# Bonus and variance products of a gated SSM/RWKV block taken in high and low parts

## The chip, the cores and the metric

One core of a Trainium2 chip runs the whole kernel. The metric is device time in microseconds (us) of one execution; it is given as the median of the runs shown. The engines are named as in the profile: PE is TensorE's matmul side and PEld its weight loads, DVE is VectorE, ACT is ScalarE, POOL is GpSimd, and SP is the queue that issues most DMAs.

## The reference

One trunk layer on x of shape 1 x 2048 x 1024 in float32:

```
h = RMSNorm(x)
[u | rwkv_in | gate_a | gate_b] = h @ W_in
o_a = S5 diagonal SSM on u, then a half-GLU
o_b = RWKV-7 time mixing on rwkv_in            (8 heads x 64)
merged = sigmoid(gate_a)*(o_a @ Wb_a) + sigmoid(gate_b)*(o_b @ Wb_b)
x = x + merged @ W_out
x = x + relu(RMSNorm(x) @ W1)^2 @ W2
out = RMSNorm(x)
```

The change touches three sums over the 64 channels of a head inside o_b:

```
kk    = k*k_k / max(norm(k*k_k over the head), 1e-12)
var   = mean((y - mean)^2 over the head);  y = (y - mean)*rsqrt(var + 64e-5)
bonus = sum(r*k*r_k over the head) * v
```

## The kernel before, in words

The kernel runs in four phases: A (norm, input projection, S5), B (RWKV, and the two gate projections beside it), C (GLU, branch merge, output projection) and D (feed-forward). Only phase B (`phase_b`, from L600) is touched. Channels lie on the 128 partitions and time on the free axis; two heads share the partitions, so a sum over a head is a product with a 128x128 block matrix of ones: `bo` (ones) or `bo64` (ones divided by 64).

Phase B cuts the sequence into 16 pieces of 128 steps. For piece s there are three generators: `elem(s)` (L669) makes decays, the normalised key and the bonus; `inv(s)` (L760) makes the triangular inverse of each 64-step chunk, with a long run of small DVE steps (L805, L807) and a trip through DRAM; `chain(s)` (L878) carries the state and finishes the output. In turn i of the outer loop `robin` (L82) goes round chain(i-2), the gate projection, elem(i) and inv(i-1), one yield of each at a time. The gate projection (`gates`, L949) is a side generator: 64 output tiles of 24 products `gp`, each tile cut by yields into four portions of six products, so that they fill PE while the recurrence waits. Its weights are split into high and low parts on the chip in the first 16 tiles (ACT cast L963 to `gwh`, POOL subtraction L964 to `gwl`), stored, and read back for the other 48.

A generator's place in the round is its priority only. The framework's scheduler puts the instructions of each engine in an order at build time, taking the earliest one that its own simulation has ready; on the chip each engine then runs its list in that order, and waits where an input is late. `pin` (L666) forbids a matmul to be placed ahead of the PE instruction written before it. The SP queue, too, runs its DMAs in the order in which they stand.

The three sums before the change:

- The norm (L716 to L730): `sq` is the square of k*k_k. ACT casts it to the reduced float32 type `F32R` (`xh`, L721), POOL makes the rest `xl` (L722), and two unpinned products with `bor`, the cast of `bo`, add up in one PSUM bank `n` (L724, L725). DVE takes reciprocals of it (L728, L730), and from these come `AR` (L732) and, on POOL, `AG` (L736), which the first products `R` of chain (L893) read.
- The bonus (L742 to L749): DVE multiplies `rm` in four pieces (L743), and one full float32 product with `bo` follows in the same yield (L745); DVE multiplies the result by v (L749).
- The variance (L924 to L934): ACT copies and squares y (L924, L926); in the next yield one full float32 product with `bo64` (L929), the square root on ACT (L930), reciprocals on DVE (L931, L933). The end of chain multiplies by the gate and stores to `ob_d` through SP (L945).

Of the kernel before, what the change touches and what calls it, by code (L numbers as in the profile page):

```python
# [11 lines left out]
F32R = mybir.dt.float32r  # L12
# [3 lines left out]
ALU = mybir.AluOpType  # L16
# [583 lines left out]
def phase_b(tc, nc, K, io, pm_d, ob_d, h_d, gt_d, gs_d, inv_d):  # L600
    V, A, P, T = nc.vector, nc.scalar, nc.gpsimd, nc.tensor
    NS = S // 128
    with ExitStack() as st:
        gt = st.enter_context(tc.tile_pool(name="b_t", bufs=1, side="right", reuse_waits="tile"))
        gw = st.enter_context(tc.tile_pool(name="b_w", bufs=1, side="right", reuse_waits="tile"))
        cp = st.enter_context(tc.tile_pool(name="b_c", bufs=1, side="right", reuse_waits="tile"))
        ep = st.enter_context(tc.tile_pool(name="b_e", bufs=1, reuse_waits="tile"))
# [10 lines left out]
        def cst(n):  # L618
            o, w = COFF[n]
            return ct[:, o - NCST_A:o - NCST_A + w]  # L620

        bo, bo64, cent = cst("bo"), cst("bo64"), cst("cent")
        bor = cp.tile([128, 128], F32R, name="bor")
        A.copy(bor, bo)
        msi = cst("msi").rearrange("p (m t) -> p m t", m=2)
        lvl = cst("lvl").bitcast(U32)
# [18 lines left out]
        def gps(n):  # L645
            return psg.tile([128, 512], F32, tag="g", name=n)
# [16 lines left out]
        def fl(a):  # L663
            return a.rearrange("p h t -> p (h t)")

        def pin(f):  # L666
            return lambda *a, **k: tc.keep_in_program_order(f(*a, **k))

        def elem(s):  # L669
            d = D[s]  # L670
            if s == 0:
# [3 lines left out]
            rm, km, vm, sig, aa = (d[n] for n in ("rm", "km", "vm", "sig", "aa"))  # L675

            def tmp(n):
                return ep.tile([128, 4, 128], F32, tag=n, name=f"{n}{s}")
# [6 lines left out]
            kt, bt = BK[:, :, 0::3, :], BK[:, :, 1:3, :]  # L685
            sq = tmp("sq")
            A.activation(fl(sq), fl(kr), ACTF.Square)
            for _ in range(3):
                yield
            e1 = tmp("e1")  # L690
            V.tensor_tensor_scan(fl(e1), rst, fl(sig), 0.0, op0=ALU.mult, op1=ALU.add)
# [24 lines left out]
            d["AR"] = AR  # L716
            V.tensor_tensor(AR[:, :, 1, :], rm, e1, op=ALU.mult)
            np_ = gps(f"n{s}")
            xh = ep.tile([128, 512], F32R, tag="xh", name=f"xh{s}")
            xl = ep.tile([128, 512], F32R, tag="xl", name=f"xl{s}")  # L720
            A.copy(xh, fl(sq))  # L721
            P.tensor_tensor(xl, fl(sq), xh, op=ALU.subtract)  # L722
            yield
            T.matmul(np_, bor, xl, start=True, stop=False)  # L724
            T.matmul(np_, bor, xh, start=False, stop=True)  # L725
            P.tensor_tensor(sig, sig, kr, op=ALU.mult)
            V.scalar_tensor_tensor(fl(kr), fl(kr), -1.0, fl(e3), op0=ALU.mult, op1=ALU.mult)
            V.reciprocal(fl(sq)[:, 0:256], np_[:, 0:256])  # L728
# [6 lines left out]
            for c in range(2):  # L735
# [4 lines left out]
                            op=ALU.mult)  # L740
            yield
            for h in range(4):  # L742
                V.scalar_tensor_tensor(rm[:, h], rm[:, h], r_k[:, h:h + 1], km[:, h], op0=ALU.mult, op1=ALU.mult)  # L743
            bp = gps(f"bo{s}")
            T.matmul(bp, bo, fl(rm), start=True, stop=True)  # L745
            P.tensor_tensor(kt, km.rearrange("p h (c t) -> p h c t", c=2), e3.rearrange("p h (c t) -> p h c t", c=2),
                            op=ALU.mult)
            bv = xp.tile([128, 4, 128], F32, tag="bv", name=f"bv{s}", bufs=3)
# [129 lines left out]
        def chain(s):  # L878
# [3 lines left out]
            for c in range(2):  # L882
                n = 2 * s + c
# [14 lines left out]
                for h in range(8):  # L898
                    T.matmul(up[uc, 64 * h:64 * h + 64], Y[uc, h, :], R[uc, 64 * h:64 * h + 64],
                             start=True, stop=True)  # L900
# [16 lines left out]
                if n < 2 * NS - 1:  # L917
                    for e in range(2):
                        er = slice(64 * e, 64 * e + 64)
                        V.tensor_tensor(S1[er, :, er], SG[er], sp[er, 0:256].rearrange("p (h t) -> p h t", h=4),  # L920
                                        op=ALU.add)
# [2 lines left out]
            A.copy(ys, yp)  # L924
            y2 = ip.tile([128, 512], F32, tag="y2", name=f"y2{s}")
            A.activation(y2, yp, ACTF.Square)  # L926
            yield
            vp = gps(f"var{s}")
            T.matmul(vp, bo64, y2, start=True, stop=True)  # L929
            A.activation(y2, vp, ACTF.Sqrt, bias=geps)  # L930
            V.reciprocal(y2[:, 0:256], y2[:, 0:256])  # L931
            yield
# [73 lines left out]
        for i in range(NS + 2):  # L1006
            robin(chain(i - 2) if i >= 2 else None, gg, elem(i) if i < NS else None,
                  inv(i - 1) if 0 <= i - 1 < NS else None)
# [812 lines left out]
@with_exitstack  # L1821
def tile_hybrid_block(ctx: ExitStack, tc: tile.TileContext, io: dict, out: bass.AP):
    nc = tc.nc
    dp = ctx.enter_context(tc.tile_pool(name="dram", bufs=1, space=DRAM))
    u_d = dp.tile([512, 8, S // 8], F32, name="u_d")
    pm_d = dp.tile([2688, S], F32, name="pm_d")
    gt_d = dp.tile([2 * DM, S], F32, name="gt_d")
    h_d = dp.tile([2, NW, 128, NK, WT], F32, name="h_d")
    inv_d = dp.tile([S // 128, 2, 64, 256], F32, name="inv_d")
    gs_d = dp.tile([16, 2, 128, NK, 128], F32, name="gs_d")  # L1830
    z_d = dp.tile([512, 8, S // 8], F32, name="z_d")
    ob_d = dp.tile([512, S], F32, name="ob_d")
    oa_d = dp.tile([512, S], F32, name="oa_d")
    x1_d = dp.tile([S, DM], F32, name="x1_d")
    xt_d = dp.tile([3, 2, 128, 4, 512], F32, name="xt_d")
    r_d = dp.tile([16, 4, 128, 2, 512], F32, name="r_d")
    if True:
        K = setup(tc, nc, ctx, io)
        phase_a(tc, nc, K, io, u_d, pm_d, h_d, z_d)
        phase_b(tc, nc, K, io, pm_d, ob_d, h_d, gt_d, gs_d, inv_d)  # L1840
        with ExitStack() as sd:
            ff = []

            def following():
                ff.extend(ff_open(tc, nc, K, io, x1_d, xt_d, r_d, sd))
                return ff[1].ahead()

            phase_c(tc, nc, K, io, z_d, oa_d, ob_d, gt_d, x1_d, xt_d, following)
            phase_d(tc, nc, K, io, x1_d, r_d, out, *ff)
# [21 lines left out]
```

## Time and profile before

| | |
|---|---|
| median of 3 runs | 3075.23 us (3069.72 to 3085.65) |
| the profiled execution's own time | 3079.11 us |
| its span in the trace | 3077.3 us |
| mean granted TensorE clock | 0.979 of full speed |
| PE / PEld busy | 95% / 75% of the span |
| DVE / ACT / POOL busy | 61% / 36% / 40% of the span |
| phase B, from the first gate product to the last | about 557 to 1364 us |

Busy PE is not PE at its peak: a matmul's modelled duration overlaps the next one's, so what a product costs a full PE is read from the distance between starts in the timeline. Times in a timeline are microseconds from the start of the span; "[1.43 <-PE var L929]" says that the engine was idle for 1.43 us before the instruction, and what released it.

### The profile page before, as it was taken

Reading aid. Unit: us, or ns where it says so; the run is one execution under the profiler, and the core shown is the slowest. Engines: PE = TensorE matmul, PEld = TensorE weight load, DVE = VectorE, ACT = ScalarE, POOL = GpSimd, SP = SyncE. Lnnn points to the kernel's source line nnn. Section 1 sums busy time; section 2 is a strip of 40 time slices with the busy share of each in tenths; the row PEclk is TensorE's granted clock in tenths of the full one; section 3 lists DMA queues with packets and bytes.
Section 4 is the critical chain, followed back from the end, with each engine's and each line's share of the span. In section 5 each row is a group of like instructions: output and inputs, shape, how many; then the busy total and the mean of one; then the engine's idle time right before and its main releaser. Section 6 shows DMA issues by size and latency. Waiting matters only on the chain.

```text
span 3077.3 us, 45569 instructions
## 1 busy us (share of the span) xinstructions
PE 2913.9 (95%) x17024; PEld 2322.5 (75%) x17024; DVE 1892.2 (61%) x3307; ACT 1119.9 (36%) x1795; POOL 1219.9 (40%) x1069
## 2 busy tenths in 40 slices
PE   7989999589999999999999989999999999999998
PEld 5757777467777777777777868887788788888887
DVE  6348876457776677535323366657655476666667
ACT  5342211233333233234445355555433342222233
POOL 3101110545334333103333335555444555555554
PEclk9999999799999999999999999999999999999999
DMA  4344444756646545467565653333533386666664
GB/s 149 95 134 134 144 141 129 228 170 186 207 143 205 163 142 180 126 176 236 192 193 170 208 186 133 109 110 115 171 110 110 115 252 153 154 155 151 151 146 148
DMA packets 331676, 486.04 MB, mean 158 GB/s; under 512 B 113344, under 2 KB 174912, under 8 KB 331456
## 3 DMA queue, kind: packets, MB, share of 16 engines
q1 hardware_dynamic: 303296, 443.29, 45.1%
q0 software_dynamic: 11520, 35.66, 6.7%
q10 hardware_dynamic: 16640, 4.20, 0.5%
q8 instruction: 134, 2.20, 0.3%
q14 instruction: 86, 0.70, 0.1%
HBM read 327.71 MB, written 147.85 MB: 155 GB/s over the span
## 4 chain that ended last, share of the span: by engine, by line
PE 54%; DVE 10%; DMA 6%; issue 5%; POOL 3%; ACT 2%; SPq 1%; POOLq 0%; DVEq 0%; ACTq 0%
PE s L121 6%; PE s L123 6%; PE s L122 6%; PE f L121 5%; PE f L123 5%; PE f L122 5%; PE gp L121 2%; PE gp L122 2%; PE gp L123 2%; DMA g<-gt_d 1%; PE o L121 1%; PE o L122 1%; PE o L123 1%; DVE YC L807 1%; DVE bl L1331 1%
## 5 line engine op out<-in xcount | busy, mean ns | idle before, releaser
L121 PE MATMUL f<-bl,w1h 128*128 128x512 f32 x896 | 354.7, 396 | 8.9 <-ACT w1h L1358 8.9
L122 PE MATMUL f<-bh,w1l 128*128 128x512 f32 x896 | 351.0, 392 | 5.8 <-POOL w1l L1362 5.7
L123 PE MATMUL f<-bh,w1h 128*128 128x512 f32 x896 | 351.9, 393 | 0.0
L121 PE MATMUL s<-w2l,ah 128*128 128x512 f32 x784 | 305.8, 390 | 2.6 <-ACT s L1599 2.6
L123 PE MATMUL s<-w2h,ah 128*128 128x512 f32 x784 | 305.7, 390 | 0.0
L122 PE MATMUL s<-w2h,al 128*128 128x512 f32 x784 | 305.5, 390 | 0.0
L1362 POOL TENSOR_TENSOR w1l<-w1r,w1h 128x512 fp32r<-128x512 f32 x122 | 175.0, 1437 | 183.4 <-ACT w1h L1358 183.0
L121 PE MATMUL gp<-gh,gwh 128*128 128x512 f32 x512 | 222.4, 434 | 22.3 <-DMA gh<-h_d 13.5
L122 PE MATMUL gp<-gh,gwl 128*128 128x512 f32 x512 | 211.9, 414 | 10.5 <-POOL gwl L964 6.9
L1358 ACT CAST w1h<-w1r 128x512 fp32r<-128x512 f32 x224 | 137.8, 620 | 204.6 <-PE f L123 143.3
L1576 POOL TENSOR_TENSOR al<-ra,ah 128x1024 fp32r<-128x1024 f32 x64 | 166.9, 2610 | 111.5 <-ACT ah L1575 111.4
L123 PE MATMUL gp<-gh,gwh 128*128 128x512 f32 x512 | 209.6, 409 | 0.0
L1606 DVE TENSOR_TENSOR c<-c,s 128x512 f32<-128x512 f32 x224 | 149.8, 684 | 90.6 <-PE s L123 90.5
L122 PEld LDWEIGHTS f<-bh,w1l 128*128 128x128 f32 x896 | 169.2, 189 | 45.5 <-POOL w1l L1362 8.9
L121 PEld LDWEIGHTS f<-bl,w1h 128*128 128x128 f32 x896 | 169.3, 189 | 45.3 <-ACT w1h L1358 10.4
L123 PEld LDWEIGHTS f<-bh,w1h 128*128 128x128 f32 x896 | 169.1, 189 | 38.3
L121 PE MATMUL p<-hl,wh 128*128 128x512 f32 x448 | 182.6, 408 | 3.6 <-ACT lo L583 3.6
L123 PE MATMUL p<-hh,wh 128*128 128x512 f32 x448 | 178.3, 398 | 0.0
L122 PE MATMUL p<-hh,wl 128*128 128x512 f32 x448 | 177.8, 397 | 0.0
L121 PEld LDWEIGHTS s<-w2l,ah 128*128 128x128 f32 x784 | 147.6, 188 | 33.6 <-ACT s L1599 3.0
L122 PEld LDWEIGHTS s<-w2h,al 128*128 128x128 f32 x784 | 147.6, 188 | 30.8
L123 PEld LDWEIGHTS s<-w2h,ah 128*128 128x128 f32 x784 | 147.5, 188 | 30.7
(382 smaller groups left out, 6763.5 us busy)
## 6 DMA issues: line engine op xcount, KB each, us to landing
w1r<-in_w_dram SPq DMA_DIRECT2D x64, 512.0 KB, 3.4
r_d<-c SPq DMA_DIRECT2D x128, 256.0 KB, 2.0
ra<-r_d SPq DMA_DIRECT2D x64, 512.0 KB, 3.3
gwl<-gs_d SPq DMA_DIRECT2D x48, 512.0 KB, 4.5
gwh<-gs_d SPq DMA_DIRECT2D x48, 512.0 KB, 4.6
ch<-r_d POOLq DMA_DIRECT2D x42, 512.0 KB, 5.5
gh<-h_d SPq DMA_DIRECT2D x64, 256.0 KB, 5.4
gt_d<-gs SPq DMA_DIRECT2D x64, 256.0 KB, 5.1
```

Of the source, the lines that this page charges most:

```text
L121: nc.tensor.matmul(ps, wh, xl, start=start, stop=False)
L122: nc.tensor.matmul(ps, wl, xh, start=False, stop=False)
L123: nc.tensor.matmul(ps, wh, xh, start=False, stop=stop)
L807: V.tensor_tensor(YC[:, 0:k, k:16], YC[:, 0:k, k:16], tv, op=ALU.add)
L1331: V.tensor_tensor(l[k], o, h[k], op=ALU.subtract)
L1358: cast = A.copy(h, o)
L1362: (P if n % 2 or edge else V).tensor_tensor(l, o, h, op=ALU.subtract)
L1576: P.tensor_tensor(l, raw[n], h, op=ALU.subtract)
L1606: V.tensor_tensor(d, d, bank, op=ALU.add if i in (4, 5, 6) else ALU.subtract)
```

## The change

The float32 products of bonus and variance become pairs of `F32R` products like the norm's, with a second cast constant `bor64`. A helper `parts` makes the high part on ACT and the low part on DVE (the norm's low part moves from POOL to DVE), and a helper `ones` issues the two products, both pinned. The three users share one buffer each for `xh` and `xl`. In elem one of three early yields goes, and one is added between the bonus's parts and its product, so that elem still has 14 yields; the steps between the two run one yield earlier. In chain the parts come in the yield of the square.

```diff
+        bor64 = cp.tile([128, 128], F32R, name="bor64")
+        A.copy(bor64, bo64)
         A.copy(bor, bo)
...
+        def parts(n, x):
+            xh = ep.tile([128, 512], F32R, tag="xh", name=f"xh{n}")
+            xl = ep.tile([128, 512], F32R, tag="xl", name=f"xl{n}")
+            A.copy(xh, x)
+            V.tensor_tensor(xl, x, xh, op=ALU.subtract)
+            return xh, xl
+
+        def ones(ps, w, xh, xl):
+            pin(T.matmul)(ps, w, xl, start=True, stop=False)
+            pin(T.matmul)(ps, w, xh, start=False, stop=True)
...
-            for _ in range(3):
+            for _ in range(2):
                 yield
             e1 = tmp("e1")
...
-            xh = ep.tile([128, 512], F32R, tag="xh", name=f"xh{s}")
-            xl = ep.tile([128, 512], F32R, tag="xl", name=f"xl{s}")
-            A.copy(xh, fl(sq))
-            P.tensor_tensor(xl, fl(sq), xh, op=ALU.subtract)
-            yield
-            T.matmul(np_, bor, xl, start=True, stop=False)
-            T.matmul(np_, bor, xh, start=False, stop=True)
+            xh, xl = parts(f"n{s}", fl(sq))
+            yield
+            ones(np_, bor, xh, xl)
...
+            xh, xl = parts(f"b{s}", fl(rm))
+            yield
             bp = gps(f"bo{s}")
-            T.matmul(bp, bo, fl(rm), start=True, stop=True)
+            ones(bp, bor, xh, xl)
...
             A.activation(y2, yp, ACTF.Square)
+            xh, xl = parts(f"v{s}", y2)
             yield
             vp = gps(f"var{s}")
-            T.matmul(vp, bo64, y2, start=True, stop=True)
+            ones(vp, bor64, xh, xl)
```

## Rows read from the trace of the kernel before

**Rows 1.** The page: engine totals, then busy tenths of PE and its clock in 40 slices.

```profile
PE 2913.9 (95%) x17024; PEld 2322.5 (75%) x17024; DVE 1892.2 (61%) x3307; ACT 1119.9 (36%) x1795; POOL 1219.9 (40%) x1069
...
PE   7989999589999999999999989999999999999998
...
PEclk9999999799999999999999999999999999999999
```

**Rows 2.** Windows: length, busy us of PE, PEld, DVE, ACT, POOL; clock, DMA, GB/s.

```profile
560.00:580.00 20.00, 6.66 (x20) 3.12 (x18) 7.28 (x7) 5.93 (x9) 10.08 (x15) 0.76 1.08 334
580.00:600.00 20.00, 9.84 (x37) 7.06 (x37) 12.02 (x15) 5.49 (x9) 18.87 (x21) 0.72 0.34 119
...
900.00:950.00 50.00, 48.29 (x536) 38.12 (x536) 35.78 (x82) 17.79 (x32) 18.64 (x26) 1.00 0.56 158
950.00:1000.00 50.00, 49.47 (x524) 39.26 (x523) 35.60 (x61) 19.77 (x33) 17.11 (x23) 1.00 0.70 225
```

**Rows 3.** Groups by line, 560 to 1345 us: the products of the three sums.

```profile
L745 PE MATMUL bo<-rm,cstb 128*128 128x512 f32 x32 | 17.7, 636 | 3.3 <-DVE ys L944 2.2 <-DVE YC L807 0.6 <-DVE sq L730 0.4
...
L929 PE MATMUL var<-y,cstb 128*128 128x512 f32 x32 | 16.3, 591 | 0.0
...
L724 PE MATMUL n<-xl,bor 128*128 128x512 f32 x16 | 7.3, 456 | 5.2 <-POOL xl L722 5.2
```

**Rows 4.** Timeline of PE around one variance product, full clock.

```profile
951.75 0.39 PE L123 MATMUL gp<-gh,gwh 128*128 128x512 f32 x1
951.98 1.02 PE L929 MATMUL var<-y,cstb 128*128 128x512 f32 x2
952.43 0.79 PE L121 MATMUL gp<-gh,gwh 128*128 128x512 f32 x1
953.06 0.40 PE L122 MATMUL gp<-gh,gwl 128*128 128x512 f32 x1
953.30 0.39 PE L123 MATMUL gp<-gh,gwh 128*128 128x512 f32 x1
```

**Rows 5.** Groups of one tile: casts and subtractions into high and low parts.

```profile
L721 ACT CAST xh<-sq x16: 617/620/623, 569.2 to 1231.1; 128x512 fp32r<-128x512 f32 x16
...
L722 POOL TENSOR_TENSOR xl<-sq,xh x16: 1257/1502/2222, 569.9 to 1233.1; 128x512 fp32r<-128x512 f32 x16
...
L572 DVE TENSOR_TENSOR xl<-sg,xh x4: 680/692/692, 137.6 to 205.4; 128x512 fp32r<-128x512 f32 x4
```

**Rows 6.** Timeline of POOL and PE at the start of phase B.

```profile
569.92 2.22 POOL L722 TENSOR_TENSOR xl<-sq,xh 128x512 fp32r<-128x512 f32 x1 [17.63 <-ACT xh L721]
...
586.62 2.04 POOL L736 TENSOR_TENSOR AG<-AR,gam 128x512 f32<-128x512 f32 x2
588.63 2.34 POOL L964 TENSOR_TENSOR gwl<-gwr,gwh 128x1024 fp32r<-128x1024 f32 x1
...
587.71 1.33 PE L893 MATMUL R<-SB,AG 128*64 128x128 f32 x5 [14.30 <-POOL AG L736]
...
591.13 0.92 PE L122 MATMUL gp<-gh,gwl 128*128 128x512 f32 x1
...
607.47 1.16 PE L667 MATMUL m<-AR,BK 64*128 64x128 f32 x16
```

**Rows 7.** Waits of 560 to 1345 us: engine, line, awaited: us, times, longest.

```profile
DVE y L931 <- ACT y L930: 21.8, 5, 9.1
...
PE U L899 <- DVE Rs L895: 1.9, 4, 0.8
```

**Rows 8.** Timeline of the square root and the reciprocal behind it, one piece.

```profile
953.03 0.69 ACT L930 ACTIVATE y<-var,geps 128x512 f32<-128x512 f32 x1 [1.43 <-PE var L929]
...
954.49 1.74 DVE L931 RECIPROCAL y<-y 128x256 f32<-128x256 f32 x1
```

**Rows 9.** Timeline of DVE and POOL where a DVE step meets a POOL one.

```profile
731.80 2.30 DVE L805 TENSOR_TENSOR yt<-NC,YC 64x64 f32<-64x64 f32 x1
734.13 0.22 DVE L807 TENSOR_TENSOR YC<-YC,yt 64x64 f32<-64x64 f32 x1
...
731.63 2.39 POOL L964 TENSOR_TENSOR gwl<-gwr,gwh 128x1024 fp32r<-128x1024 f32 x1 [2.32 <-ACT gwh L963]
```

**Rows 10.** Timeline of the SP queue at the end of phase B.

```profile
1352.05 0.37 SPq L945 DMA_DIRECT2D ob_d<-ys  x1
1352.53 0.93 SPq L959 DMA_DIRECT2D gwh<-gs_d  x1
1353.50 0.45 SPq L959 DMA_DIRECT2D gwl<-gs_d  x1
```

## The prediction, made before the change was run

> **What bounds the kernel now.** I read the page first: PE is busy 95% of the span, in nearly every slice nine tenths or more, at a granted clock that is near full [rows 1]. So the question for each edit is whether it gives or takes time on PE. Then I cut phase B into windows. It has two parts. In its first 40 us PE works 6.66 and 9.84 us of 20 at a clock of 0.76 and 0.72, while POOL is busy 18.87 of 20 in the second window: here POOL sets the pace. Later, in the two windows from 900 to 1000, PE is busy 48.3 and 49.5 us of 50 at a clock of 1.00, DVE about 36, ACT 18 to 20, POOL 17 to 19 [rows 2]. There the gate products fill PE, so PE time that is saved is time of the kernel, and PE that waits costs the same.
>
> **What goes from PE.** A full float32 product shows as two records, so 16 pieces give 32 of them for each of bonus and variance, of 590 to 640 ns; the norm's half is one record of 456 ns [rows 3]. Records overlap, so I price by starts. Gate products of the same shape start 0.23 us apart (951.75 to 951.98; 953.06 to 953.30). The variance product starts at 951.98; the second gate product behind it starts at 953.06, and the first one's share of that is 0.23, so variance held PE from 951.98 to 952.83, or 0.85 us [rows 4]. Two reduced products hold it for 0.46. The saving is 0.39 us, times 32 products: **-12.5 us**. Where PE is idle anyway (the first window) it is worth nothing, but that touches one or two products of 32.
>
> **What is added elsewhere.** ACT gets 32 casts of 0.62 us, 20 us. DVE gets 48 subtractions of 0.69 us (priced by the same operation in phase A), 33 us, and POOL loses 16 of 1.50 us, 24 us [rows 5]. Neither ACT (18 to 20 of 50 busy) nor DVE (36 of 50) comes near being full by that: a piece takes some 44 us, as the 16 casts from 569.2 to 1231.1 show [rows 5], and DVE gains 2.1 us in each, so 36 of 50 becomes 38.4. Throughput hides these; the cover is PE's own work, and without it they would cost their own 33 us on DVE. The cast of the second constant is one small ACT instruction before the first gate product, where PE waits for loads: nothing. Nothing is added to or moved past the SP and POOL queues except as said below; the pieces issue the same DMAs.
>
> **The wait that is added.** In the norm and the variance PE now needs a low part that stands in DVE's list, behind whatever DVE was given before it, and PE stands still while it waits, with gate products behind it. The trace has no such wait for them: variance shows 0.0 idle, since only ACT stood ahead of it, and the norm's 5.2 is the one at the start [rows 3]. I bound it from rows in which PE does wait for DVE. Low end: the 32 products U behind Rs lost 1.9 us in all, 0.06 each [rows 7]. High end: how late DVE comes to work that is ready. At one piece the square root was done at 953.72 and DVE took it up at 954.49, 0.77 us later [rows 8]; in only 5 of 16 pieces did DVE wait for ACT there at all, so in the others it came late [rows 7]. Nearest is the bonus product itself, which already waits for DVE's multiply in its own yield: 3.3 us in 16, 0.21 each [rows 3]. I take 0.21 for the 32 norm and variance products: **+6.6 us** (1.9 to 25). The bonus keeps its 3.3: its parts come one yield earlier and its product stays where it was, with 1.3 us more work in a round of nearly 3 us (44 over 15 rounds). Moving the middle of elem one yield earlier changes no sum of work; a gain or a loss of a microsecond or two is possible, and I take zero. The shared buffers put the norm's cast behind the variance product of the piece two before it; before, it could run far ahead. That is inside the 0.21.
>
> **The start.** POOL runs without a gap from 569.92 to the low part of the second gate weights, 588.63 to 590.97, and the first gate product that reads it starts at 591.13. The norm's first low part, 2.22 us, lies in that run [rows 6] and goes: **-2.2 us**. Against it, the norm's products are now pinned behind the gate products written before them, so `AR` and `AG` come later; PE stood 14.3 us for `AG` anyway [rows 6], and the inverse's first products, which read `AR`, start only at 607.47 [rows 6]. Bounds for the stage: -4.3 us, if the gate weights now also pass the 2.04 us of `AG` in POOL's list, and +4 us, if the later `AG` is what PE meets next.
>
> **The end.** The last variance takes a cast and a subtraction more, 1.3 us, and 0.39 less on PE. The store of its output heads the SP queue, ahead of the last gate weights [rows 10], so **+0.9 us** passes on to the last gate products.
>
> **Sum.** -12.5 + 6.6 - 2.2 + 0.9 = -7.2 us. The profiled execution took 3079.1 us (its span and 1.8 around it); this makes it 3071.9. It is 3.9 above the median, and the same sum on the median of 3075.2 gives **3068**. A change of 0.5%, 15.4 us, is about what a measurement of this kernel can tell from none: the bounds are 3059.9 and 3090.6. With the waits at their low end and the start at its better end the sum is -14; with the waits three times as long and the start neutral it is +8. The main case's own range is 3061 to 3083.
>
> **A rule on the other side.** A DVE step on 64x64 took 2.30 us at 731.80 while a POOL subtraction ran from 731.63 for 2.39, and 0.22 us right after it [rows 9]. So a DVE instruction with two inputs can be held for most of a POOL one. The Trainium skill says why, SBUF — State Buffer, section SBUF: two separate sides: VectorE with two SBUF inputs and GpSimd share a port pair that one of them locks for a whole instruction. The row agrees. By that rule a subtraction that starts on DVE while POOL is at work waits for the rest of it, and moving it to DVE can hurt; this is the slower rival below.
>
> **The rivals.** *Slower:* the low parts are late, above all the variance's, which falls into the run of small DVE steps of inv that POOL stretches. Its price: if each of 48 products waits as long as in rows 8, 0.77 us, that is 37 us, less 12.5 and 2.2: +22, or 3097. It decides from (15.4 + 12.5 + 2.2) / 48 = 0.63 us a product. For it: DVE came late in 11 of 16 pieces [rows 7]. Against: one wait lets DVE catch up, so the next is shorter; 16 POOL subtractions that hold DVE go; and other products that need DVE lose far less. 0.17.
>
> *Faster:* waits stay at 0.06 each, as for U, 1.9 us, and the first stage of phase B, where PE idles on POOL, gives 4.3 us and the norm's second low part 1.3: -12.5 + 1.9 - 5.6 = -16, or 3059. For it: the idle time of the first windows is large [rows 2], and the list of POOL loses what stood in the way. Against: it needs each term at its good end. 0.27.
>
> *It shows nothing:* the change doesn't do what the price of a product says, because the order of the lists shifts and the 0.39 us comes back as waits somewhere: 3075, between 3068 and 3082. For it: the saving is 0.4% of the time, and the waits that take it need only be 0.4 us for each of 32 products. 0.22.
>
> **How the numbers follow.** The main case has 0.34, and lies within 0.5%, as does the third rival. Faster by over 0.5%: 0.27. Slower: 0.18, the rival and a hundredth for a worse start. Within: 0.55. The range reaches from 3052, past the centre of the faster case, to 3095, near the centre of the slower one; about 0.05 lies below and 0.12 above.
>
> **What would show it.** Bonus, variance and norm products of 390 ns in pairs, 16 of each half, with starts 0.23 us apart; POOL without its 16 subtractions; 48 DVE subtractions near 0.69 us. PE's waits for a low part between 2 and 10 us in all. The first gate product with the second low weights at 589 us or before. I am wrong if these waits pass 20 us, if the low parts take over 1 us on DVE on the average, or if the first stage moves by more than 5 us either way.

## The result, and the profile after

The median after the change is 3102.19 us (5 runs, 3094.35 to 3104.62), against 3075.23 before: a ratio of 1.0082, 95% interval 1.0066 to 1.0099. The kernel became slower by about 25 us (the ratio on 3075; the two medians lie 27 apart). The forecast was 3068 us, and 3102 lies above its range of 3052 to 3095.

The profiled execution took 3102.2 us, with a span of 3100.3 (before 3077.3). The page, as in [rows 1]:

```profile
PE 2926.5 (94%) x17024; PEld 2331.4 (75%) x17024; DVE 1917.5 (62%) x3355; ACT 1137.1 (37%) x1828; POOL 1217.6 (39%) x1053
...
PE   7989999589899999999999989999999999999998
...
PEclk9999999889999998999999999999999999999999
```

No engine got fuller by much: DVE went from 61% to 62%, ACT from 36% to 37%. PE is still the engine that bounds the kernel. Slices are 77.5 us long, and phase B lies in the 8th to the 18th: there its busy row has an 8 more (the 11th), and its clock row has 8 in three slices, where before it had one 7. (PE's count of records is the same, since a full product already showed as two.)

Where the 23 us of span come from is seen in the tile of the gate products, first and last start. The first two lines are the kernel before, the others the kernel after:

```profile
L121 PE MATMUL gp<-gh,gwh x512: 387/395/799, 556.6 to 1363.4; 128*128 128x512 f32 x171
L122 PE MATMUL gp<-gh,gwl x512: 387/393/918, 557.2 to 1363.6; 128*128 128x512 f32 x171
```

```profile
L121 PE MATMUL gp<-gh,gwh x512: 387/397/797, 557.9 to 1391.5; 128*128 128x512 f32 x171
L122 PE MATMUL gp<-gh,gwl x512: 386/394/795, 558.4 to 1391.8; 128*128 128x512 f32 x171
```

Phase B starts 1.3 us later and ends 28.1 us later (1391.5 against 1363.4); the phases behind it then take 5 us less. So all of it arises in phase B. Cut into four windows, with the columns of [rows 2], the kernel before:

```profile
610.00:800.00 190.00, 166.06 (x1572) 127.40 (x1571) 133.37 (x251) 64.36 (x105) 94.19 (x108) 0.92 0.60 189
800.00:1000.00 200.00, 194.79 (x2140) 153.76 (x2140) 144.47 (x289) 75.20 (x129) 79.58 (x110) 1.00 0.58 176
1000.00:1200.00 200.00, 188.44 (x1937) 144.44 (x1936) 142.92 (x310) 63.78 (x110) 78.24 (x109) 0.97 0.55 163
1200.00:1400.00 200.00, 193.50 (x1756) 151.18 (x1755) 107.34 (x204) 63.43 (x109) 38.45 (x35) 0.97 0.54 156
```

and the kernel after:

```profile
610.00:800.00 190.00, 161.80 (x1465) 121.34 (x1464) 133.68 (x250) 65.44 (x108) 86.78 (x96) 0.92 0.55 177
800.00:1000.00 200.00, 191.81 (x2173) 151.71 (x2170) 146.02 (x303) 75.99 (x133) 82.93 (x112) 0.99 0.59 175
1000.00:1200.00 200.00, 186.84 (x1845) 143.03 (x1845) 140.72 (x306) 70.62 (x122) 67.88 (x98) 0.96 0.50 149
1200.00:1400.00 200.00, 187.39 (x1807) 144.60 (x1806) 107.61 (x221) 55.17 (x101) 32.94 (x38) 0.93 0.49 147
```

Read the third number, PE's busy time, and the clock behind POOL's column. PE is busy 742.8 us of 790 before and 727.8 after: 15 us more idle. And its clock is lower in three of four windows, by 0.01, 0.01 and 0.04. Busy time times clock, window by window, is 718 us before and 692 after, so PE did about 26 us less work in the same stretch, 15 from standing still and the rest from the clock. (The last window of before holds some 36 us of the next phase.) The change made PE's work smaller; PE stood still more and ran slower.

The groups of the three sums, with the forms kept apart, 560 to 1385 us, answer to [rows 3] and [rows 5]. Behind the bar: busy us, mean ns of one, then the idle time of the engine just before them and what ended it.

```profile
L669 PE MATMUL var<-xlv,bor 128*128 128x512 f32 x16 | 7.8, 487 | 11.3 <-DVE xlv L676 11.3
L669 PE MATMUL n<-xln,bor 128*128 128x512 f32 x16 | 7.4, 463 | 7.4 <-DVE xln L676 7.0
L669 PE MATMUL bo<-xlb,bor 128*128 128x512 f32 x16 | 7.0, 437 | 1.9 <-DVE xlb L676 1.9
...
L676 DVE TENSOR_TENSOR xlb<-rm,xhb 128x512 fp32r<-128x512 f32 x16 | 14.8, 926 | 0.0
L676 DVE TENSOR_TENSOR xlv<-y,xhv 128x512 fp32r<-128x512 f32 x16 | 10.9, 680 | 10.6 <-ACT xhv L675 10.6
L676 DVE TENSOR_TENSOR xln<-sq,xhn 128x512 fp32r<-128x512 f32 x16 | 10.4, 649 | 1.3 <-ACT xhn L675 1.3
...
L675 ACT CAST xhb<-rm 128x512 fp32r<-128x512 f32 x16 | 9.9, 620 | 32.1 <-PE n L669 31.6 <-DVE y L946 0.6
```

The products are cheap, as said, and the subtractions are near 0.68 us. What is new stands in the last column of the first line: the variance product, which showed 0.0 idle before [rows 3], now waits 11.3 us for its low part. The last line shows the shared buffer: in all, ACT stands 31.6 us before the bonus's casts until the norm's product has let the buffer go. PE's largest waits of the same stretch, as in [rows 7], read line, awaited, total, times, longest:

```profile
PE gp L121 <- ACT gwh L976: 18.5, 3, 12.1
PE gp L122 <- POOL gwl L977: 13.6, 5, 8.1
PE var L669 <- DVE xlv L676: 11.3, 11, 3.6
PE n L669 <- DVE xln L676: 7.0, 3, 4.0
```

The first two, 32.1 us, belong but for 0.5 us to the first 110 us of phase B. There they take the place of the 14.3 us for `AG` and the norm's 5.2 [rows 3, rows 6], and of 13.3 for the same two in the kernel before: 32.8 in all. One variance product in the timeline of ACT, DVE and PE, at full clock:

```profile
959.60 0.60 ACT L938 ACTIVATE y<-y 128x512 f32<-128x512 f32 x1
960.24 0.62 ACT L675 CAST xhv<-y 128x512 fp32r<-128x512 f32 x1
...
961.64 0.39 PE L123 MATMUL gp<-gh,gwh 128*128 128x512 f32 x1
...
962.01 0.21 DVE L819 TENSOR_TENSOR YC<-YC,yt 64x60 f32<-64x60 f32 x1
962.15 0.68 DVE L676 TENSOR_TENSOR xlv<-y,xhv 128x512 fp32r<-128x512 f32 x1
...
962.88 0.50 PE L669 MATMUL var<-xlv,bor 128*128 128x512 f32 x1 [0.85 <-DVE xlv L676]
...
963.22 0.39 PE L669 MATMUL var<-xhv,bor 128*128 128x512 f32 x1
...
963.45 0.40 PE L121 MATMUL gp<-gh,gwh 128*128 128x512 f32 x1
```

The cast is done at 960.86. DVE is in the small steps of `inv` and takes the subtraction at 962.15, 1.3 us later. PE issued its last gate product at 961.64 and stands 0.85 us, with gate products behind the variance in its list that need nothing from DVE. This repeats in 11 of 16 pieces.

### The profile page after: what moved, and what is told of

Read it like the earlier page. It is cut to its first block, busy times and chain, and to the rows that moved or that the text cites. A ratio compares the mean times of both kernels' runs of the same rounds, so it can differ in the third digit from the quotient of the medians.

```text
span 3100.3 us, 45670 instructions
## 1 busy us (share of the span) xinstructions
PE 2926.5 (94%) x17024; PEld 2331.4 (75%) x17024; DVE 1917.5 (62%) x3355; ACT 1137.1 (37%) x1828; POOL 1217.6 (39%) x1053
## 4 chain that ended last, share of the span: by engine, by line
PE 51%; DVE 7%; DMA 5%; issue 4%; POOL 3%; ACT 2%; SPq 1%; POOLq 0%; DVEq 0%; ACTq 0%
PE f L121 6%; PE f L123 6%; PE f L122 6%; PE s L122 6%; PE s L123 6%; PE s L121 6%; DMA g<-gt_d 2%; PE gp L121 2%; PE gp L122 1%; PE gp L123 1%; DMA wor<-in_wout_dram 1%; DVE YC L819 1%; PE b L121 1%; PE b L122 1%; PE b L123 1%
## 5 line engine op out<-in xcount | busy, mean ns | idle before, releaser
L1375 POOL TENSOR_TENSOR w1l<-w1r,w1h 128x512 fp32r<-128x512 f32 x122 | 181.6, 1491 | 180.6 <-ACT w1h L1371 174.0
```

Source lines behind the costliest of these rows:

```text
L1375: (P if n % 2 or edge else V).tensor_tensor(l, o, h, op=ALU.subtract)
```

## Experiments

All were timed in five rounds beside the kernel before on the same chip; ratios are to that kernel, with their 95% interval. Diffs are against the kernel named.

**The variance back as one full product** (against the kernel after).

```diff
-            xh, xl = parts(f"v{s}", y2)
-            ones(vp, bor64, xh, xl)
+            T.matmul(vp, bo64, y2, start=True, stop=True)
```

> The changed kernel with the variance product put back to one full float32 product; bonus and norm keep their parts on VectorE. Theory 1 (the loss is TensorE standing for the variance's low part, 11.3 us of waits in the changed kernel, which VectorE makes inside the run of small steps of the inverse): those waits go and 6.2 us of saving on the products go with them; with the clock lost after such waits given back too, 3075 to 3088. Theory 2 (the lists were put in another order, and the order costs, whichever product it is): it stays at 3095 to 3105.

Measured 3080.75 us, 1.0021 (1.0008 to 1.0033). Three quarters of the loss go with the variance's parts, though its product costs PE more again. This is within theory 1.

**The variance alone in parts** (against the kernel before).

```diff
+            A.copy(xh, y2)
+            V.tensor_tensor(xl, y2, xh, op=ALU.subtract)
...
-            T.matmul(vp, bo64, y2, start=True, stop=True)
+            pin(T.matmul)(vp, bor64, xl, start=True, stop=False)
+            pin(T.matmul)(vp, bor64, xh, start=False, stop=True)
```

> The kernel before with the variance product alone taken in parts, cast on ScalarE and low part on VectorE, products pinned; bonus, norm and yields as before. Theory 1: most of the loss is here already, 3082 to 3100, with 8 to 20 us of TensorE waiting for the variance's low part. Theory 2: whatever the new order gives, with few waits for that low part; by the price of the products alone 3069.

Measured 3083.64 us, 1.0034 (1.0021 to 1.0047). PE waits 6.5 us for the low part, in 9 pieces, less than the 8 that theory 1 asked for, and about what the 16 cheaper products give back. Yet the time is 10 us longer. By itself the variance's part of the change loses, but less than it takes in the whole change.

**One more yield between the variance's parts and its product** (against the kernel after).

```diff
             xh, xl = parts(f"v{s}", y2)
             yield
+            yield
             vp = gps(f"var{s}")
```

> The changed kernel with one more yield between the variance's parts and its product, so that the pinned product stands behind one more portion of gate products. Theory 1: the waits for the variance's low part fall from 11.3 us to 3 or less and the time to 3080 to 3092. Theory 2: no gain beyond 5 us, unless by accident of the order.

Measured 3110.22 us, 1.0119 (1.0101 to 1.0137). The wait only shrinks from 11.3 to 8.0 us, and PE now waits 14.0 us for the inverse's `X`. Neither theory foresaw this. I read it so: more room for the low part makes chain longer, and that costs more than the wait gives back; only the waits show it.

**The norm's low part back on POOL** (against the kernel after).

```diff
-            xh, xl = parts(f"n{s}", fl(sq))
+            xh, xl = parts(f"n{s}", fl(sq), P)
```

> The changed kernel with the norm's low part made by GpSimd as before; bonus and variance parts stay on VectorE. If the norm's move to VectorE is the cost, the 7.0 us of waits for its low part go and the time is 3085 to 3095; by theory 1 the variance's waits remain and the time stays at 3093 or above.

Measured 3087.31 us, 1.0043 (1.0029 to 1.0057): half the loss, where theory 1 said 3093 or above. The norm's wait falls from 7.0 to 2.9 us, but the variance's, whose code is the same, from 11.3 to 8.1:

```profile
PE var L669 <- DVE xlv L676: 8.1, 8, 3.6
```

**The variance takes its high part twice, and its low part isn't made** (against the kernel after).

```diff
-            xh, xl = parts(f"v{s}", y2)
+            A.copy(xh, y2)
...
-            ones(vp, bor64, xh, xl)
+            ones(vp, bor64, xh, xh)
```

> The changed kernel, but the variance product takes the high part twice and no low part is made (the low part is left out of the sum, the high one counts double): two reduced products as in the change, without VectorE's subtraction and without the wait for it. Theory 1 (the wait for VectorE is the loss): no waits for VectorE at the variance, 3072 to 3083. Theory 2 (the order of the lists): stays above 3090.

Measured 3083.63 us, 1.0035 (1.0025 to 1.0046). The wait at the variance is gone; PE now waits 9.3 us for the norm's low part and 10.6 for the inverse's `X` (2.8 in the change).

**The same, but DVE makes the low part, and nobody reads it** (against the kernel after).

```diff
-            ones(vp, bor64, xh, xl)
+            ones(vp, bor64, xh, xh)
```

> The same as the run before it, but VectorE still makes the variance's low part, which no product reads: VectorE's 11 us without TensorE's wait; the lists stand almost as in the changed kernel. If the wait of TensorE is the loss, 3075 to 3087, near the run before it; if VectorE's added work is the loss, through what comes late behind it, 3090 to 3102, near the changed kernel.

Measured 3079.82 us, 1.0027 (1.0013 to 1.0041). This is the nearest test of the variance's wait. DVE does all its new work, the products are as cheap as in the change, and PE's wait for the low part is gone. The two intervals lie apart: 1.0082 falls to 1.0027, some 17 us. And against the run before it, the 16 subtractions themselves cost nothing that can be told. But the lists are not those of the change. With one operand fewer to wait for, the scheduler ordered anew: of DVE's 1102 instructions of phase B, 116 have changed places in the trace (47 of 1054 when only the pins were added to the kernel before, 201 when only the yields were moved). So the 17 us are the wait and another order together. The waits that are left, PE in 560 to 1385 us:

```profile
PE n L669 <- DVE xln L676: 13.4, 9, 4.0
```

The norm's low part now is the one that comes late, by 6.4 us more than in the change.

**All three low parts on POOL** (against the kernel after).

```diff
-            V.tensor_tensor(xl, x, xh, op=ALU.subtract)
+            P.tensor_tensor(xl, x, xh, op=ALU.subtract)
```

> The changed kernel with all three low parts made by GpSimd (48 subtractions of 1.3 to 1.7 us), VectorE freed of them. Theory 1: GpSimd is not in the run of small steps, so waits for the low parts fall from 20 us to 5 to 12 and the time is 3075 to 3092. If the parts cost by their latency alone, whoever makes them, it stays at 3095 to 3110.

Measured 3097.25 us, 1.0082 (1.0068 to 1.0097), the same as the change. PE waits 11.7 us for the norm's part and 7.1 for the variance's, now for POOL. So theory 1 failed here. The two waits sum to 18.8 us, as in the change (18.3): moving the subtraction out of DVE's list only moved the wait.

**The bonus alone in parts, with the change's yields, pins and shared buffers** (against the kernel after).

```diff
-            xh, xl = parts(f"n{s}", fl(sq))
+            xh, xl = parts(f"n{s}", fl(sq), P)
...
-            ones(vp, bor64, xh, xl)
+            T.matmul(vp, bo64, y2, start=True, stop=True)
```

> The changed kernel with the variance as one full product and the norm's low part on GpSimd as before: of the change the bonus in parts, the pinned products, the yields and the shared buffers stay. If the two VectorE low parts of norm and variance are the whole loss, the bonus's saving of 6.2 us shows: 3066 to 3074. If pins, yields or shared buffers cost by themselves, 3075 to 3090.

Measured 3084.87 us, 1.0044 (1.0027 to 1.0061). With no low part from DVE on PE's path but the bonus's, it is still slower than before. So the late parts are not the whole loss. This run differs from the one with the norm's low part on POOL (1.0043) in the variance alone, and takes the same time: there PE waited 8.1 us for the variance's part, here not at all, with products that cost 4 to 5 us more.

**The change without pins** (against the kernel after).

```diff
-            pin(T.matmul)(ps, w, xl, start=True, stop=False)
-            pin(T.matmul)(ps, w, xh, start=False, stop=True)
+            T.matmul(ps, w, xl, start=True, stop=False)
+            T.matmul(ps, w, xh, start=False, stop=True)
```

> The changed kernel with the six products of the three sums not pinned. If the pins cost (a product may not pass the gate products written before it, nor they be held by it), the time falls by 5 to 20 us to 3080 to 3095; by the theory of VectorE's late low parts it stays within 6 us of the changed kernel, with 8 us or more of waits for the variance's low part.

Measured 3089.81 us, 1.0066 (1.0054 to 1.0078). The variance still waits 12.5 us, and the wait for `AG` at the start is back (16.2 us). So the pin isn't what makes the variance wait: left free, the scheduler puts its product where it comes too early all the same.

**Only the pins** (against the kernel before).

```diff
-            T.matmul(bp, bo, fl(rm), start=True, stop=True)
+            pin(T.matmul)(bp, bo, fl(rm), start=True, stop=True)
```

and likewise for the norm's two products and the variance's.

> The kernel before, only with its norm, bonus and variance products pinned. If the pins are what is left of the loss once the variance's wait is away (some 8 us), 3077 to 3085; if not, 3066 to 3076.

Measured 3077.82 us, 1.0026 (1.0016 to 1.0036). The start of phase B looks as in the change (19.0 us for `gwh`, 13.9 for `gwl`), and PE waits 10.8 us for `X`, against 4.7 before.

**Only the yields** (against the kernel before): two early ones for three, and one between the bonus's multiply and its full product.

```diff
-            for _ in range(3):
+            for _ in range(2):
                 yield
...
+            yield
             bp = gps(f"bo{s}")
```

> The kernel before, only with the yields of the change: two early ones in place of three, and one between the bonus's multiply and its full product. If the earlier middle of elem is what is left of the loss, 3077 to 3085; if not, 3066 to 3076.

Measured 3099.39 us against 3068.98, 1.0098 (1.0085 to 1.0111). Both forecasts were far below this. No work is added, no product is cheaper, and it costs as much as the whole change. Its windows show the same picture, idle time and a lower clock, in the columns used above:

```profile
610.00:800.00 190.00, 164.04 (x1508) 123.47 (x1506) 131.97 (x243) 64.47 (x105) 91.91 (x106) 0.91 0.57 181
800.00:1000.00 200.00, 191.81 (x2116) 149.77 (x2116) 142.50 (x288) 70.83 (x123) 78.68 (x111) 0.97 0.58 175
1000.00:1200.00 200.00, 181.55 (x1814) 141.07 (x1813) 132.30 (x275) 61.94 (x108) 72.39 (x101) 0.92 0.47 140
```

PE's waits name what became late; the kernel before shows 4.7 us for the first of these:

```profile
PE P L667 <- DVE X L818: 12.5, 6, 5.0
...
PE P L864 <- DVE X L858: 8.0, 5, 3.6
```

`X` is the transposed block that the inverse's products `P` read. I read it so: with the middle of elem one yield earlier, its DVE work takes the places of inv's in DVE's list, and inv comes late. In the change itself, which has the same yields, this isn't seen: there PE waits 2.8 and 1.0 us for `X`.

**The change with the yields of before** (against the kernel after).

```diff
-            for _ in range(2):
+            for _ in range(3):
                 yield
...
             xh, xl = parts(f"b{s}", fl(rm))
-            yield
             bp = gps(f"bo{s}")
```

> The changed kernel with the yields of before: three early ones, and the bonus's product in the yield of its parts. If the yields cost, 3085 to 3095; if they pay, the bonus's product waits for its low part as the variance's does, 5 to 12 us more of waits, and 3105 to 3118.

Measured 3092.51 us, 1.0078 (1.0065 to 1.0092); the interval overlaps the change's. PE waits 2.9 us for `X`, as in the change, and longer for the variance:

```profile
PE var L669 <- DVE xlv L676: 13.4, 11, 3.6
```

So the yields that cost 30 us in the kernel before cost nothing in the change that this can tell. Nor is it that either cause alone brings the whole loss: the change with the low part of the variance unread has the same yields, and lost only 0.27%.

**Each yield by itself** (against the kernel before). The one between the bonus's multiply and its product:

```diff
                 V.scalar_tensor_tensor(rm[:, h], rm[:, h], r_k[:, h:h + 1], km[:, h], op0=ALU.mult, op1=ALU.mult)
+            yield
             bp = gps(f"bo{s}")
```

> The kernel before with one yield more between the bonus's multiply and its full product; nothing else. If the place of the bonus product in the round is what costs (theory: elem grows to 15 yields, so its tail and the inverse of the next piece shift against the gate portions), most of the +0.98% of both yields shows: 1.006 to 1.011. If the middle of elem one yield earlier is what costs, this stays within 0.998 to 1.003.

Measured 3088.25 us, 1.0048 (1.0033 to 1.0062). Here phase B's gate products end no later (1361.4 us), but the last chain does (SP issues its store at 1375.1 us, against 1352.1 before [rows 10]); the loads of the next phase stand behind that store in SP's list, and PE waits. PE's largest wait from 1355 to 1420 us, where the kernel before shows 2.3 for the same line:

```profile
PE g L121 <- ACT wgh L1093: 20.0, 1, 20.0
```

And two early yields for three:

```diff
-            for _ in range(3):
+            for _ in range(2):
                 yield
```

> The kernel before with two early yields in elem in place of three; nothing else, so all of elem behind them runs one yield earlier. If the middle of elem one yield earlier is what costs, by putting its DVE work ahead of the small steps of inv: 1.006 to 1.011, with PE's wait for the inverse's X near 20 us in place of some 3. If the other yield costs: 0.998 to 1.003. If each order other than that of before costs a little, both this and the run before it give 1.002 to 1.005.

Measured 3087.35 us, 1.0037 (1.0023 to 1.0052), with waits for `X` of 6.1 and 11.4 us. That is 17.5 us for `X` in all, against 5.2 before. Neither yield is the one; each costs, and both together cost about their sum.

**Both causes away: yields of before, and low parts made but not read** (against the change with the yields of before). First the variance's alone:

```diff
-            ones(vp, bor64, xh, xl)
+            ones(vp, bor64, xh, xh)
```

> The change with the yields of before; the variance's second product takes the high part twice and its low part is made but not read (this leaves the low part out of the sum). If the late low part of the variance is the only cause left once the yields are back: 1.0078 less 0.0055, or 1.002, and with norm and bonus as they are still waits of some 10 us for them. If the products' saving shows: 0.996 to 1.000. If a third cause stands behind both, it stays at 1.005 or above.

Measured 3087.13 us, 1.0047 (1.0034 to 1.0061), nearest to a third cause; the forecast of 1.002 failed. PE waits for no low part but once for the bonus's (1.2 us); its one new wait is 11.8 us for `wgh` at the entry of the next phase (2.3 before). Then those of all three sums:

```diff
-            pin(T.matmul)(ps, w, xl, start=True, stop=False)
+            pin(T.matmul)(ps, w, xh, start=True, stop=False)
```

> The change with the yields of before; all three sums take the high part twice, and the low parts are made but not read (this leaves them out of the sums). PE waits for no low part, only for the casts on ACT. If waits and yields are the whole cause, the saving of 12.5 us shows: 0.995 to 0.999. If pins, casts or the order of the lists cost by themselves: 1.000 to 1.006.

Measured 3089.57 us, 1.0048 (1.0032 to 1.0064). PE waits for no low part, the products are cheap, the yields are those of before, and the saving still doesn't show. Against the change with the yields of before, the waits for low parts were worth 0.3%. The rest, half a percent over the kernel before, stays with the pins (0.26% by themselves), the casts, the shared buffers and the order of the lists; these runs don't tell them apart.

**The bonus alone, unpinned, with the yields of before, the norm's part on POOL** (against the kernel before).

```diff
+            xh, xl = parts(f"b{s}", fl(rm))
...
-            T.matmul(bp, bo, fl(rm), start=True, stop=True)
+            T.matmul(bp, bor, xl, start=True, stop=False)
+            T.matmul(bp, bor, xh, start=False, stop=True)
```

> The kernel before with only the bonus in parts, unpinned, in the yield of its multiply, with buffers shared with the norm, whose low part stays on POOL; variance as a full product. If the saving on PE counts where no low part is late: 16 times 0.39 is 6.2 us, less a wait for the bonus's parts of some 3, 0.997 to 1.000. If each other order of the lists costs by itself, as pins alone (+0.26%) and either yield (+0.37%, +0.48%) did: 1.002 to 1.006.

Measured 3082.67 us, 1.0020 (1.0008 to 1.0032). PE waits 7.1 us for the bonus's low part, where the full product waited 3.3 for the multiply [rows 3]. Of all versions tried none is faster than the kernel before; this one and the change with a full variance are the nearest.

**Each full product issued twice** (against the kernel before).

```diff
             T.matmul(vp, bo64, y2, start=True, stop=True)
+            T.matmul(vp, bo64, y2, start=True, stop=True)
```

and likewise for the bonus.

> The kernel before with each full product of bonus and variance issued twice into the same bank (the second one overwrites the first); no other engine gets work. If PE's time at these products is time of the kernel: 32 times 0.85 is 27 us, 1.007 to 1.010, and up to 1.014 with what another order costs. If PE would have stood idle there anyway: 1.000 to 1.004, and the saving of the change was never to be had in full.

Measured 3089.57 us, 1.0047 (1.0031 to 1.0064): 14.5 us (9.5 to 19.7) for 27 us of PE work, and what another order costs or gives is in these 14.5. The trace shows where a part of the rest went: from the first gate product to the last PE stands 58.0 us of 816.6, against 68.7 of 807.2 before. So PE's time at these products looks worth about half of itself.

## Why the prediction was wrong

**What bounds the kernel: right.** PE does, and the loss is seen as PE's idle time and clock.

**What goes from PE: right in size, wrong in worth.** Priced as before (from the start of a product to that of the second gate product behind it, less 0.23), ten variance products at full clock before the change each held PE 0.86 us. After it the bonus's pair holds 0.47 (four of the six places where two gate products follow it), but the variance's 0.57 in most pieces: there the second product starts 0.34 us after the first (962.88 to 963.22), not 0.23, in all eleven pieces with a wait and in three without. That makes 16 x 0.39 and 16 x 0.29, or 10.9 us in place of 12.5. "PE time that is saved is time of the kernel" was read from windows in which PE is busy 48 to 49 of 50 us. The worth seems less: doubling the products cost 14.5 us for 27, so about half of the term. That run adds work and doesn't take it away, so the half is an estimate.

**What is added elsewhere: right.** The subtractions take 0.65 to 0.93 us, and making the variance's, with nobody reading it, cost nothing that can be told.

**The wait that is added: the term was mis-sized.** I took 0.21 us for each of the 32 norm and variance products, 6.6 us, by the row of the bonus; it was 11.3 + 7.0 = 18.3, or 0.57 each, within my bounds of 1.9 to 25 but in their upper half. With the bonus's 1.9 it is 20.2, past the 20 that I had named as the sign of being wrong. The bonus was the wrong nearest row. Its multiply stands in elem; the variance's subtraction stands among the small steps of inv, like the square root's reciprocal, which DVE took up 0.77 us late [rows 8]. That row was for the same piece of code, and was kept for a rival. With the sizes that were measured and the start at nothing, the sum is -10.9 + 18.3, or +7, and +13 if the products are worth half. The kernel lost 25, so 12 to 18 us stand in no term of mine.

**The start: right in its first step, but it gave nothing.** POOL and PE of the kernel after:

```profile
586.90 2.34 POOL L977 TENSOR_TENSOR gwl<-gwr,gwh 128x1024 fp32r<-128x1024 f32 x1
```

```profile
589.29 0.79 PE L122 MATMUL gp<-gh,gwl 128*128 128x512 f32 x1 [8.14 <-POOL gwl L977]
...
591.59 0.63 PE L669 MATMUL n<-xln,bor 128*128 128x512 f32 x1
```

The first product with the second low weights starts at 589.29 in place of 591.13, 1.8 us earlier (I said 2.2), and the norm stands behind it. It doesn't last: ACT's copy of the eighth gate tile comes at 664.4 us against 663.1 before, as late as phase B began, and that of the 22nd at 877 against 866.

**The end: not tested by itself.** SP issued the store of the last output at 1380.42 us, 28.4 after that of before [rows 10], as late as all of phase B.

**"Moving the middle of elem one yield earlier changes no sum of work; a gain or a loss of a microsecond or two is possible, and I take zero": a term put at nothing for a reason that doesn't hold.** The yields alone cost 0.98% in the kernel before, 30 us, more than every priced term. It is true that the sum of work stays; what moves is the order of the lists, there with `X` coming late. But that isn't their price in the change. Taking them back there gave 0.04% (1.0082 to 1.0078), and with the variance's low part unread it was the version with the change's yields that came out nearer to before (1.0027 against 1.0047, intervals that overlap). The same holds for the pins, which I weighed at the start only: 0.26% by themselves, and 0.16% when taken out of the change, also with intervals that overlap. So what failed is the step that an edit of the order has a price of its own, zero or another, that can be added to the rest.

**The rivals.** The slower one named the right place, "above all the variance's, which falls into the run of small DVE steps", but its price, 0.77 us for each of 48 products, was nearly twice what was seen: 11.3 + 7.0 + 1.9 = 20.2 us, or 0.42 each, below the 0.63 from which it was to decide. By waits alone it would not have ended slower. Its port rule is seen in one piece of the kernel after, POOL, DVE and PE:

```profile
687.85 2.34 POOL L977 TENSOR_TENSOR gwl<-gwr,gwh 128x1024 fp32r<-128x1024 f32 x1 [0.97 <-POOL SG L902]
688.00 2.27 DVE L817 TENSOR_TENSOR yt<-NC,YC 64x60 f32<-64x60 f32 x1
...
690.68 0.67 DVE L676 TENSOR_TENSOR xlv<-y,xhv 128x512 fp32r<-128x512 f32 x1
```

```profile
691.41 0.50 PE L669 MATMUL var<-xlv,bor 128*128 128x512 f32 x1 [3.56 <-DVE xlv L676]
```

A small step that takes 0.2 us elsewhere takes 2.27 beside POOL's subtraction, and the variance's low part behind it comes 2 us later: the variance's longest wait, 3.56 us. This agrees with the Trainium skill, SBUF — State Buffer, section SBUF: two separate sides. It explains that wait, not the usual one: ten of the eleven sum to 7.7 us. And with the parts made by POOL the time was the same. The third rival, that the order of the lists gives the saving back as waits, is nearest to what the runs show, at a third of the price: it gave back the 12.5 us, while 25 more were lost.

**What is shown, and what stays open.** Four pairs of versions differ in how the variance is taken (the full product also needs no cast and no subtraction) and in the order that the scheduler made of it:

| where | low part read | not read | gain | PE's wait that went |
|---|---|---|---|---|
| the change; part made, unread | 1.0082 | 1.0027 | 17 us | 11.3 us |
| the change; full product | 1.0082 | 1.0021 | 19 us | 11.3 us |
| yields of before; part made, unread | 1.0078 | 1.0047 | 10 us | 13.4 us |
| norm's part on POOL; full product | 1.0043 | 1.0044 | 0 us | 8.1 us |

A full product costs 4 to 5 us more in all, so the wait itself was worth some 17, 23, 10 and 4 us: an estimate of 13 on the average for waits of 11, with a spread larger than itself. That the variance's late low part costs is shown by three pairs of four. Its share of the 25 us is not. The norm does the same: its part back on POOL won 12 us in the change, and lost 7 with the variance as a full product (1.0021 to 1.0044).

Open is the rest. The pins alone, each yield alone, the bonus alone, and the low parts unread with the yields of before cost 0.2 to 0.5% each. In some of them one operand comes late, but not the same one: `X` with two early yields (17.5 us against 5.2), `wgh` at the next phase with the late yield (20.0 against 2.3). Where no wait stands out, as with all low parts unread, PE stands 74.5 us in phase B against 68.7 and its clock there is 0.94 against 0.96. That the order of before is a good one among many would explain it, but nothing here tests that. The shared buffers, for which ACT stands 31.6 us, weren't tried by themselves: they stay a rival.

## What to carry to other kernels

A cheaper product on a busy engine can be worth less than its time if it takes an operand from another engine's list, because an engine that runs in order then stands for that list with independent work behind it. Price the wait by the row of the code among which the operand is made, not by the product most like it. And where a scheduler makes the lists anew from each program, a moved yield, a pin or an operand fewer is a change of order too, and its price depends on the rest: the same yields cost 30 us in one version and nothing in another. Don't put it down at zero, and don't price a cause from one pair of versions; take the same edit out in several.

## What the runs showed that was not expected

**A wait can cost again through the clock, and the clock falls without one too.** Windows around the wait at 691.41 us in the kernel after (length, PE busy, PEld, DVE, ACT, POOL, clock):

```profile
684.00:692.00 8.00, 4.44 (x37) 3.43 (x32) 7.53 (x18) 3.60 (x6) 4.54 (x4) 0.99 0.27 100
692.00:696.00 4.00, 4.00 (x12) 3.10 (x12) 3.61 (x9) 1.91 (x3) 0.69 (x1) 0.60 0.35 62
696.00:700.00 4.00, 4.00 (x22) 3.03 (x21) 1.40 (x1) 0.59 (x1) 0.00 (x0) 1.00 0.78 232
```

PE stands 3.56 us of the first window, and in the next 4 us the granted clock is 0.60, mostly the lower of its two levels, 1.2 GHz; PE is busy all the time, and gate products start 0.43 us apart (693.40 to 693.83), where at 2.4 GHz they start 0.23 apart. At 0.60 of the clock 4 us of work lose 1.6, on top of the 3.56. That waits let the clock fall, and that the time behind them is paid at half speed, agrees with the Trainium skill, TensorE: Matmul & The Clock Gate, section HAM oscillation — how this bites in real kernels. Over all executions the mean clock is 0.976 with the change and 0.979 with the variance's low part unread, so clock can be a part of why that run won more than the wait.

But little of it stands right behind that wait. Of the ten falls of the clock from 600 to 1390 us in the kernel after, one begins behind a wait for the variance's low part and two behind one for the norm's. The four longest, of 10 to 14 us, stand elsewhere, and one of them has no wait just before it (columns as above):

```profile
1077.00:1084.00 7.00, 7.00 (x122) 5.37 (x121) 5.74 (x9) 1.93 (x4) 3.83 (x4) 1.00 0.79 233
1084.00:1095.00 11.00, 11.00 (x102) 9.09 (x95) 5.13 (x10) 3.73 (x6) 5.24 (x11) 0.53 0.28 81
```

By the profile PE is busy for all 7.00 us before the clock falls, with many small products of the recurrence among the gate products, and for the 11 us after it. Why the clock fell there is open. Nor does the mean clock of a profiled execution order the versions: it is 0.974 to 0.976 in the four with a ratio of 1.0082 or more, and also in eight others, down to 1.0021.
